# Second inverse's first levels on GpSimd, small products at other steps, opening and end in another order

## The chip, the cores and the metric

The kernel runs on one core of one Trainium2 chip. The metric is the device time of one execution in microseconds (us). The kernel before took 1145.91 us in the median of three runs. A profile is one execution recorded by the hardware; its own time stands in the table below.

Engines go by these names: PE is TensorE (matmuls; PEld is its weight load), DVE is VectorE, ACT is ScalarE, POOL is GpSimd, SP is SyncE, which here only issues transfers. Each engine takes its instructions in the order of its queue; an instruction that waits holds up all that stand behind it on the same engine.

## What is computed

The reference is a model of two layers over 256 tokens of width 2048. The first layer is an RWKV-7 mixer with 32 heads of size 64, the second a sparse attention with 16 heads. Cut to what matters here:

```python
def wkv7_scan(r, w, k, v, a, b):
    def step(S, inp):
        r_t, w_t, k_t, v_t, a_t, b_t = inp
        sa = jnp.einsum('bhvk,bhk->bhv', S, a_t)
        S = S * w_t[:, :, None, :] + sa[..., None] * b_t[:, :, None, :] + v_t[..., None] * k_t[:, :, None, :]
        return S, jnp.einsum('bhvk,bhk->bhv', S, r_t)

def rwkv7_mixer(u, ...):
    xx = token_shift(u) - u
    mixed = u[None] + xx[None] * mu[:, None, None, :]
    rkvz = jnp.einsum('nbtd,nde->nbte', mixed[:4], w_rkvz)
    r, k, v, z = rkvz[0], rkvz[1], rkvz[2], rkvz[3]
    ...
    o = wkv7_scan(rh, heads(decay), kh, vh, -kk, kk * ah)
    ...
    o = (o + bonus) * jax.nn.silu(z)
    return o.astype(u.dtype) @ w_o, v

def reference(x, ...):
    ...
    return rmsnorm(h, final_g)
```

The kernel does not scan token by token. It cuts the 256 tokens into four chunks of 64. Within a chunk the recurrence is a triangular system, so a unit triangular matrix of 64 x 64 has to be inverted for each head and chunk. The kernel inverts its two 32 x 32 diagonal blocks and puts the rest together in the scan.

## The kernel before

All large products are exact to about fp32: each weight and each activation is split into a high part and a low part, and three products are added. The class Weights does this for the weights. SP loads a raw piece (wraw, five buffers), ScalarE copies it to the high part (whi, line 211), VectorE, or GpSimd for some late pieces, takes the difference (wlo, line 190). There are AHEAD + 2 = 5 buffers of whi and wlo, so pieces are made up to five steps ahead, and a new one waits until TensorE has freed a buffer. The activations' parts (mx) are made in split_into: a copy on ScalarE (line 426), a subtraction on VectorE (line 427).

The order of the work: the opening loads x, norms and turns it (lines 357 to 500); then come the values (phase_v), the first block of the gate z, sixteen key blocks (phase_k), the second gate block (phase_z1), the third and fourth (late_z), then the scan over eight units of four heads with the r projection and the output projection laid between, then the second layer, and its last product with the final norm (phase_bo, finish).

A gate block is 512 columns and 16 steps over k; in a step rows_step (lines 583 to 589) issues six matmuls of 512 columns. Each key block j needs small work afterwards: k_norm (a column sum on TensorE at line 732, a root on GpSimd, a copy on ScalarE at line 738), k_turn (two transposes at line 745, then VectorE lines 750 and 751 and GpSimd line 756) and k_close (sixteen small products at line 765, copies on ScalarE, lines 768 and 769, and three stores from SP to the tensor abd). In phase_k these run at step KP = 3 of a later block. What is left after the last key block runs in phase_z1 at the steps of the tuple ZP: at its first step k_close(13), k_turn(14), k_norm(15); at its second k_close(14), k_turn(15); at its third k_close(15).

The inverses are in inverse_load and inverse_ops. There are two, b = 0 for key blocks 0 to 7 and b = 1 for 8 to 15, and each partition holds one 32 x 32 block. inverse_load brings abd to the tile invA, for b = 1 from GpSimd's queue. inverse_ops makes a list of instructions: the identity into invT (memsets, for b = 1 on GpSimd), the 2x2 blocks' corners (a copy of 16 elements), and then levels that double the block: 2 and 4 by products and sums over broadcast views, 8 and 16 by dot products (each a product and a sum over the last axis, on VectorE) after a turn of the upper blocks by ScalarE copies. At the end invT goes to tnd and its transpose to yvd, from where the scan loads them. In the profile all these instructions carry line 824, where op() stands.

What sets the order: a small planner (Sched) walks the phases with a clock of costs and lets generators, the mixes and stage_t among them, run beside them at due times; stage_t issues the inverse's instructions with the pauses given in op(). stage_t(1) starts when key block 15 is closed and the first inverse is out. From this order a scheduler then makes each engine's queue by readiness and rank, except in parts where an engine keeps the written order: the opening (VectorE, ScalarE, GpSimd, TensorE), the key blocks and phase_z1 (TensorE alone), and the scan (TensorE, VectorE, ScalarE, GpSimd, SP). The scan's order is made by the class Deal, which also lays in what is left of the second inverse's list then.

The r mixes (mx from xx) wait for phase_z1's end: their scale is the tile gate, which GpSimd sets to 1.0 there (line 656), after the block's last use of it.

At the end accumulate adds the product to the residual (line 1967), ScalarE squares and sums it (line 1969), and the column's weight is multiplied in (line 1970): on GpSimd for the first four parts of the columns, on VectorE for the last. finish takes the root (VectorE lines 1553 and 1554, GpSimd line 1555), scales the four parts and stores them.

Of the kernel before, what the change touches and what calls it, by code (L numbers as in the profile page):

```python
# [13 lines left out]
OP = mybir.AluOpType  # L14
# [54 lines left out]
HS, HSK = 300, 4  # L69
W1D, CXG = 5, 1  # L70
KPO = 3
KP, ZP = 3, (0, 6, 12)
AUX = {2: ("B0",), 3: ("G",), 4: ("B1",), 5: ("Y",), 7: ("A0",), 8: ("A1",), 9: ("T",)}
AUXL = {2: ("B0",), 3: ("G",), 4: ("B1",), 5: ("Y",), 8: ("T",), 9: ("A0",), 10: ("A1",)}
OPEN = (32, "G", "B0", "B1", 3, "Y", 3, "A0", 2, "A1", 8)
# [149 lines left out]
def hybrid_kernel(ctx: ExitStack, tc: tile.TileContext, a: dict, out: bass.AP):  # L225
# [99 lines left out]
    for ph in QZ:  # L325
        if ph < 10:
            c0 = 128 * QB0[ph]
# [28 lines left out]
    def load_x(tt, c0, c1):  # L356
        nc.sync.dma_start(xt[:, tt, c0:c1], a["x"][0, tt * 128:(tt + 1) * 128, c0:c1])
# [2 lines left out]
    load_x(0, 0, 1024)  # L360
    load_x(0, 1024, 2048)
    load_x(1, 0, 1024)
    load_x(1, 1024, 1536)
    load_x(1, 1536, 2048)
    W.load(1)
    nc.sync.dma_start(prow[0:16, 0, :], g16(a["a_norm_g"][0]))
    nc.sync.dma_start(prow[16:112, 0, :], a["a_mu"][0].rearrange("i (j p) -> (i j) p", p=128))
    nc.sync.dma_start(prow[112:128, 0, :], g16(a["a_k_k"][0]))
    W.load(3)

    def C(name):
# [87 lines left out]
    def scale(tt, c0, c1):  # L459
        sl = xt[:, tt, c0:c1]  # L460
        V.tensor_scalar(sl, sl, rs[:, tt, 1:2], None, op0=OP.mult)
# [7 lines left out]
    if True:  # L469
        turned_x = [accp("tp") for _ in range(2)]  # L470
        S.activation(sq[:, 0:1], half[:, 0:1], AF.Square)
        keep_warm(WARM[0])
        square(0, 0, 1024, 0, S)
        square(0, 1024, 1536, 1, V)
        square(0, 1536, 2048, 2, V)
        rstd0(0)
        square(1, 0, 1024, 0, S)
        square(1, 1024, 1536, 1, V)
        scale(0, 0, 512)
        for kp in range(2):  # L480
            turn_half(turned_x, 0, kp)
        keep_warm(WARM[1])
        square(1, 1536, 1792, 2, V)
        square(1, 1792, 2048, 3, S)
        PE.transpose(pp[:, 0:128], prow[:, 0, :], ident)
        keep_warm(WARM[2])
        rstd0(1)
        W.hold = True
        W.ensure(PRE)
        V.tensor_copy(prm0, pp[:, 0:128])  # L490
        scale(1, 0, 256)
        turn_half(turned_x, 1, 0)
        keep_warm(WARM[3])
        W.low(1)
        scale(1, 256, 512)
        turn_half(turned_x, 1, 1)
        px = turned_x[0]
        for k in range(2):
            norm_x(k, px[:, 256 * k:256 * k + 256], V)
            m = mixed_in("v", k)  # L500
            W.low(1)
            split_into(m, "v", k)
        W.hold = False
# [311 lines left out]
    def inverse_ops(b, A):  # L815
        ops = []
        Tm = late.tile([128, 32, 32], F32, name="invT", bufs=1)
        M1 = late.tile([128, 16, 16], F32, name="invM", bufs=1)
        M2 = late.tile([128, 16, 16], F32, name="invM2", bufs=1)
        X = late.tile([128, 1024], F32, name="invX", bufs=1)  # L820
        PE, V, S, G = Ranked(nc.tensor, "stE"), Ranked(nc.vector, "stE"), Ranked(nc.scalar, "stE"), Ranked(nc.gpsimd, "stE")

        def op(eng, n, fn, *args, pause=0.0, **kw):
            ops.append((eng, n, lambda: fn(*args, **kw), pause))

        flat = Tm.rearrange("p a b -> p (a b)")
        fa = A.rearrange("p a b -> p (a b)")
        op("G" if b else "V", 1024, (G if b else V).memset, Tm, 0.0, pause=500.0)
        op("G" if b else "V", 32, (G if b else V).memset, flat[:, 0::33], 1.0)
        op("V", 16, V.tensor_copy, flat[:, 32::66], fa[:, 32::66], pause=1000.0)  # L830

        def view(t, r0, c0, n, step, rows, colsn, tr=False):
            base = t[:, r0, c0:c0 + 1]
            ap = [list(base.ap[0]), [step * 33, n], [32, rows], [1, colsn]]
            return bass.AP(tensor=base.tensor, offset=base.offset, ap=ap)

        for lv in (2, 4):
            n = 32 // (2 * lv)
            size = n * lv * lv
            m1 = M1.rearrange("p a b -> p (a b)")[:, :size].rearrange("p (n i j) -> p n i j", n=n, i=lv)  # L840
            m2 = M2.rearrange("p a b -> p (a b)")[:, :size].rearrange("p (n i j) -> p n i j", n=n, i=lv)
            x = X[:, :size].rearrange("p (n i j) -> p n i j", n=n, i=lv)
            sh = [128, n, lv, lv]
            for m, first, second in ((m1, lambda k: view(A, lv, k, n, 2 * lv, lv, 1), lambda k: view(Tm, k, 0, n, 2 * lv, 1, lv)),
                                     (m2, lambda k: view(Tm, lv, lv + k, n, 2 * lv, lv, 1), lambda k: m1[:, :, k:k + 1, :])):
                for k in range(lv):
                    op("V", size, V.tensor_tensor, m if k == 0 else x, first(k).to_broadcast(sh), second(k).to_broadcast(sh),
                       op=OP.mult, pause=0.0 if k else DT * 0.25)
                    if k:
                        op("V", size, V.tensor_tensor, m, m, x, op=OP.add, pause=DT * 0.25)  # L850
            op("V", size, V.tensor_copy, view(Tm, lv, 0, n, 2 * lv, lv, lv), m2)

        def dot(out, aa, bb, hb, kk):
            x = X[:, :hb * hb * kk].rearrange("p (i j k) -> p i j k", i=hb, j=hb)
            for i0, i1 in [(0, 4), (4, 8)] if b and hb == 8 else [(0, hb)]:
                sh = [128, i1 - i0, hb, kk]
                n = (i1 - i0) * hb * kk
                op("V", n, V.tensor_tensor, x[:, i0:i1], aa[:, i0:i1, None, :].to_broadcast(sh),
                   bb[:, None, :, :].to_broadcast(sh), op=OP.mult)
                op("V", n, V.tensor_reduce, out[:, i0:i1], x[:, i0:i1], axis=AX.X, op=OP.add,  # L860
                   pause=DT * (0.75 if hb == 8 else 1.0))

        TT = M2.rearrange("p a b -> p (a b)")
        rows = X.rearrange("p (a b) -> p a b", b=32)
        M1f = M1.rearrange("p a b -> p (a b)")
        for lv in (8, 16):
            hb = lv // 2
            Tt = TT[:, :lv * 16].rearrange("p (j k) -> p j k", k=lv)
            Mt = M1f[:, :lv * lv].rearrange("p (j k) -> p j k", k=lv)
            corner = [2 * lv * g for g in range(32 // (2 * lv))]  # L870
            for g, o in enumerate(corner):
                op("S", lv * lv, S.activation, Tt[:, g * lv:g * lv + lv],
                   Tm[:, o:o + lv, o:o + lv].rearrange("p k j -> p j k"), AF.Copy)
            for g, o in enumerate(corner):
                for j0 in (0, hb):
                    for i0 in (0, hb):
                        dot(Mt[:, j0:j0 + hb, i0:i0 + hb].rearrange("p j i -> p i j"),
                            A[:, o + lv + i0:o + lv + i0 + hb, o + j0:o + lv],
                            Tt[:, g * lv + j0:g * lv + j0 + hb, j0:lv], hb, lv - j0)
                for i0 in (0, hb):  # L880
                    for j0 in (0, hb):
                        dot(Tm[:, o + lv + i0:o + lv + i0 + hb, o + j0:o + j0 + hb],
                            Tm[:, o + lv + i0:o + lv + i0 + hb, o + lv:o + lv + i0 + hb],
                            Mt[:, j0:j0 + hb, 0:i0 + hb], hb, i0 + hb)
        op("G", 0, nc.gpsimd.dma_start, tnd[b], Tm)
        for i in range(0, 32, 8):
            op("S", 256, S.activation, rows[:, i:i + 8, :], Tm[:, :, i:i + 8].rearrange("p a b -> p b a"), AF.Copy, pause=700.0)
        op("G", 0, nc.gpsimd.dma_start, yvd[b], rows)
        return ops
# [1075 lines left out]
    def accumulate(tt, ps, c0, cols, i):  # L1965
        hv = tailed(tt, c0, cols)
        V.tensor_tensor(hv, ps, hv, op=OP.add)
        scr = fin.tile([128, 512], F32, name="scr", bufs=2)
        S.activation(scr[:, :cols], hv, AF.Square, accum_out=ssh[:, tt, i:i + 1])
        (G if i < 4 else V).tensor_tensor(hv, hv, tailed(2, c0, cols), op=OP.mult)  # L1970

    def finish(tt):
        rstd(ssh, rsh, tt)
        for i, (c0, c1) in enumerate(((0, 512), (512, 1024), (1024, 1536), (1536, 2048))):
            hv = tailed(tt, c0, c1 - c0)
            if i % 2:
                S.activation(hv, hv, AF.Copy, scale=RS[tt])
            else:
                V.tensor_scalar(hv, hv, RS[tt], None, op0=OP.mult)
            nc.sync.dma_start(out[0, tt * 128:(tt + 1) * 128, c0:c1], hv)  # L1980
# [63 lines left out]
```

## Time and profile before

| what | value |
|---|---|
| time, three runs | 1145.91, 1143.14, 1145.94 us |
| time of the profiled execution | 1146.2 us |
| its span | 1144.4 us |
| mean granted clock of TensorE | 0.989 |
| VectorE, line 190 (wlo), all forms | 616 instructions, 447.3 us |
| ScalarE, line 211 (whi), all forms | 664 instructions, 401.3 us |
| window 260 to 270 us: TensorE, VectorE, GpSimd busy | 9.31, 9.83, 6.14 us |
| window 290 to 300 us: the same | 10.00, 9.78, 2.25 us |
| window 320 to 330 us: the same | 10.00, 8.81, 9.51 us |

How to read it: the span is the time between the first and the last instruction; the execution's time has a little around it. The page has the busy time of each engine and its share of the span. A timeline has the start, the duration, the engine and the line, what is written and from what, and in brackets the idle time before it and who ended it; rows with "x3" are several instructions merged. A window has for each engine the busy microseconds and the number of instructions, then the clock granted to TensorE (1.00 is full speed), the busy share of the transfer engines and GB/s. A row of waits has who waited for whom, the total in us, how often, and the longest. A row of a group has busy time and mean duration in ns, then idle time before it.

### The profile page before, as it was taken

The page shows a single profiled execution, that of the slowest core. Times are in us where ns is not written, and L with a number is a line of the kernel's source. Part 1 is how long each engine was busy: PE and PEld are TensorE (multiplying, and loading weights), DVE is VectorE, ACT ScalarE, POOL GpSimd, SP SyncE. Part 2 cuts the span into 40 slices and gives each one's busy share as a digit, 9 for nine tenths or more (in the row PEclk, how much of TensorE's full clock was granted, in tenths as well). Part 3 has the DMA queues.
Part 4 walks back from the last instruction along what each step waited for, and adds up shares of the span by engine and source line. Part 5 has one row for each costly group of instructions (what it writes and reads, how often), then busy time and mean ns, then how long its engine had stood idle before and what let it go on. Part 6 is the DMA issues. An engine that isn't in the chain of part 4 may idle for free.

```text
span 1144.4 us, 24519 instructions
## 1 busy us (share of the span) xinstructions
PE 1107.3 (97%) x8880; PEld 939.5 (82%) x8880; DVE 869.0 (76%) x1806; ACT 716.1 (63%) x1696; POOL 367.2 (32%) x465
## 2 busy tenths in 40 slices
PE   8999999998999999999999999999999999999996
PEld 7778899987778777777778878787889988898786
DVE  6999976689786997768666876674576888988564
ACT  5667688866745456566556766564656666666553
POOL 1400057766252556653010010100333435352212
PEclk9999999998989999999999999999999999999999
DMA  6558878876898958864457758585656453848552
GB/s 218 174 190 236 247 203 256 241 219 208 245 271 255 237 159 247 211 171 134 131 179 234 225 164 284 160 292 167 188 148 162 122 146 102 203 114 278 164 186 106
DMA packets 239033, 225.35 MB, mean 197 GB/s; under 512 B 58053, under 2 KB 185333, under 8 KB 238912
## 3 DMA queue, kind: packets, MB, share of 16 engines
q1 hardware_dynamic: 233472, 216.65, 64.5%
q0 software_dynamic: 5440, 7.14, 2.4%
q8 instruction: 70, 1.15, 0.5%
q14 instruction: 51, 0.42, 0.1%
HBM read 200.48 MB, written 23.10 MB: 195 GB/s over the span
## 4 chain that ended last, share of the span: by engine, by line
PE 77%; DVE 9%; DMA 4%; issue 4%; POOL 3%; ACT 2%; SPq 0%; ACTq 0%; POOLq 0%; DVEq 0%
PE bank L587 12%; PE bank L589 12%; PE bank L586 12%; PE bank L1337 5%; PE bank L611 5%; DVE wlo L190 3%; PE bank L612 3%; PE bank L241 2%; PE bank L605 2%; PE bank L606 2%; PE bank L607 2%; PE bank L1340 2%; PE pair L1359 2%; PE pair L1361 1%; PE pair L1360 1%
## 5 line engine op out<-in xcount | busy, mean ns | idle before, releaser
L190 DVE TENSOR_TENSOR wlo<-wraw,whi 128x512 fp32r<-128x512 f32 (+2 forms) x616 | 447.3, 741 | 162.4 <-ACT whi L211 159.4
L211 ACT ACTIVATE whi<-wraw 128x512 fp32r<-128x512 f32 (+2 forms) x664 | 401.3, 620 | 241.4 <-PE bank L589 93.0
L587 PE MATMUL bank<-wlo,mx 128*128 128x512 f32 (+3 forms) x576 | 217.4, 379 | 7.4 <-DVE wlo L190 6.5
L589 PE MATMUL bank<-whi,mx 128*128 128x512 f32 (+3 forms) x576 | 215.6, 377 | 0.0
L586 PE MATMUL bank<-whi,mx 128*128 128x512 f32 (+3 forms) x576 | 187.9, 379 | 2.1 <-ACT mx L426 0.9
L587 PEld LDWEIGHTS bank<-wlo,mx 128*128 128x128 f32 x576 | 109.4, 190 | 26.2 <-DVE wlo L190 8.5
L586 PEld LDWEIGHTS bank<-whi,mx 128*128 128x128 f32 x576 | 108.4, 190 | 20.0 <-ACT whi L211 1.5
L589 PEld LDWEIGHTS bank<-whi,mx 128*128 128x128 f32 x576 | 109.3, 190 | 16.7 <-POOL mx L1926 0.4
L1337 PE MATMUL bank<-mx,whi 128*128 128x512 f32 x256 | 102.1, 430 | 0.0
L190 POOL TENSOR_TENSOR wlo<-wraw,whi 128x512 fp32r<-128x512 f32 (+2 forms) x48 | 63.0, 1314 | 110.8 <-ACT whi L211 90.1
L611 PE MATMUL bank<-mx,whi 128*128 128x512 f32 x240 | 86.6, 397 | 0.0
L605 PE MATMUL bank<-mx,whi 128*128 128x256 f32 (+1 forms) x288 | 83.0, 288 | 0.3 <-ACT mx L426 0.3
L606 PE MATMUL bank<-mx,whi 128*128 128x256 f32 (+1 forms) x288 | 81.4, 283 | 0.0
L607 PE MATMUL bank<-mx,wlo 128*128 128x256 f32 (+1 forms) x288 | 81.3, 282 | 0.0
L587 PE MATMUL bank<-wlo,kvh 128*128 128x512 f32 x192 | 76.9, 401 | 0.0
L589 PE MATMUL bank<-whi,kvl 128*128 128x512 f32 x192 | 76.1, 396 | 0.0
L612 PE MATMUL bank<-mx,wlo 128*128 128x256 f32 x256 | 70.6, 285 | 0.2 <-DVE wlo L190 0.2
L1340 PE MATMUL bank<-mx,wlo 128*128 128x256 f32 x256 | 70.7, 284 | 0.0
L586 PE MATMUL bank<-whi,kvh 128*128 128x512 f32 x192 | 67.4, 396 | 0.0
L1337 PEld LDWEIGHTS bank<-mx,whi 128*128 128x128 f32 x256 | 48.0, 189 | 10.6
L605 PEld LDWEIGHTS bank<-mx,whi 128*128 128x128 f32 (+1 forms) x288 | 54.2, 188 | 1.3 <-ACT mx L426 0.7
L607 PEld LDWEIGHTS bank<-mx,wlo 128*128 128x128 f32 (+1 forms) x288 | 54.2, 188 | 0.8 <-DVE wlo L190 0.2
(350 smaller groups left out, 2301.9 us busy)
## 6 DMA issues: line engine op xcount, KB each, us to landing
wraw<-in_a_w_rkvz_dram SPq DMA_DIRECT2D x128, 512.0 KB, 5.2
wraw<-in_kv_w_dram SPq DMA_DIRECT2D x48, 512.0 KB, 4.5
wraw<-in_b_w_in_dram SPq DMA_DIRECT2D x40, 512.0 KB, 4.3
wraw<-in_a_w_o_dram SPq DMA_DIRECT2D x32, 512.0 KB, 4.6
wraw<-in_b_w_o_dram SPq DMA_DIRECT2D x32, 512.0 KB, 4.1
spd<-sp SPq DMA_DIRECT2D x16, 642.0 KB, 5.4
wraw<-in_b_w_in_dram SPq DMA_DIRECT2D x24, 384.0 KB, 3.3
spl<-spd SPq DMA_DIRECT2D x14, 642.0 KB, 7.2
```

The source lines that it names most:

```text
L190: eng.tensor_tensor(lv, src, hv.bitcast(F32), op=OP.subtract)
L211: self.nc.scalar.activation(hv, src, AF.Copy)
L586: PE.matmul(o, mh[:, ts], wh[:, 0, :], start=k == ends[0], stop=False)
L587: PE.matmul(o, mh[:, ts], wl[:, 0, :], start=False, stop=False)
L589: PE.matmul(o, ml[:, ts], wh[:, 0, :], start=False, stop=k == ends[1])
L605: PE.matmul(o, wh[:, s, :], mh, start=k == 0 and first, stop=False, **kw)
L606: PE.matmul(o, wh[:, s, :], ml, start=False, stop=False, **kw)
L607: PE.matmul(o, wl[:, s, :], mh, start=False, stop=k == NK - 1, **kw)
L611: PE.matmul(o, wh[:, s, :], joint[nm, k], start=k == 0, stop=False, **kw)
L612: PE.matmul(o[:, :T], wl[:, s, :], mh, start=False, stop=False, **kw)
L1337: both = lambda: PE.matmul(o, wh[:, s, :], joint["r", k], start=k == 0, stop=k == NK - 1)
L1340: PE.matmul(o[:, :T], wl[:, s, :], mixed["r", k][0], start=False, stop=False)
```

## The change

It has four parts. ZP goes from steps (0, 6, 12) to (3, 8, 13) of the second gate block. In inverse_ops the first copy and all of levels 2 and 4 take the engine el/eng: GpSimd for b = 1, VectorE for b = 0 as before. In the opening the three parameter loads (prow) go ahead of the last two loads of x, the first weight load is no longer issued by itself ahead of them, and the scaling of the second token half's first columns stands ahead of the copy of the turned parameters (prm). At the end, the last part's weight is multiplied in after the root's VectorE instructions and not before them.

```diff
-KP, ZP = 3, (0, 6, 12)
+KP, ZP = 3, (3, 8, 13)
...
     load_x(1, 0, 1024)
-    load_x(1, 1024, 1536)
-    load_x(1, 1536, 2048)
-    W.load(1)
     nc.sync.dma_start(prow[0:16, 0, :], g16(a["a_norm_g"][0]))
     nc.sync.dma_start(prow[16:112, 0, :], a["a_mu"][0].rearrange("i (j p) -> (i j) p", p=128))
     nc.sync.dma_start(prow[112:128, 0, :], g16(a["a_k_k"][0]))
+    load_x(1, 1024, 1536)
+    load_x(1, 1536, 2048)
     W.load(3)
...
         W.ensure(PRE)
+        scale(1, 0, 256)
         V.tensor_copy(prm0, pp[:, 0:128])
-        scale(1, 0, 256)
         turn_half(turned_x, 1, 0)
...
         op("G" if b else "V", 32, (G if b else V).memset, flat[:, 0::33], 1.0)
-        op("V", 16, V.tensor_copy, flat[:, 32::66], fa[:, 32::66], pause=1000.0)
+        el, eng = ("G", G) if b else ("V", V)
+        op(el, 16, eng.tensor_copy, flat[:, 32::66], fa[:, 32::66], pause=1000.0)
...
                 for k in range(lv):
-                    op("V", size, V.tensor_tensor, m if k == 0 else x, ...
+                    op(el, size, eng.tensor_tensor, m if k == 0 else x, ...
                        op=OP.mult, pause=0.0 if k else DT * 0.25)
                     if k:
-                        op("V", size, V.tensor_tensor, m, m, x, op=OP.add, pause=DT * 0.25)
-            op("V", size, V.tensor_copy, view(Tm, lv, 0, n, 2 * lv, lv, lv), m2)
+                        op(el, size, eng.tensor_tensor, m, m, x, op=OP.add, pause=DT * 0.25)
+            op(el, size, eng.tensor_copy, view(Tm, lv, 0, n, 2 * lv, lv, lv), m2)
...
-        (G if i < 4 else V).tensor_tensor(hv, hv, tailed(2, c0, cols), op=OP.mult)
+        weigh = lambda: (G if i < 4 else V).tensor_tensor(hv, hv, tailed(2, c0, cols), op=OP.mult)
+        if i < 4:
+            weigh()
+        else:
+            last[tt] = weigh
+
+    last = {}
 
     def finish(tt):
         rstd(ssh, rsh, tt)
+        last[tt]()
```

More of the change, by code (lines that the diff above doesn't have):

```diff
@@ L846, in inverse_ops @@
                 for k in range(lv):
-                    op("V", size, V.tensor_tensor, m if k == 0 else x, first(k).to_broadcast(sh), second(k).to_broadcast(sh),
+                    op(el, size, eng.tensor_tensor, m if k == 0 else x, first(k).to_broadcast(sh), second(k).to_broadcast(sh),
                        op=OP.mult, pause=0.0 if k else DT * 0.25)
                     if k:
-                        op("V", size, V.tensor_tensor, m, m, x, op=OP.add, pause=DT * 0.25)
-            op("V", size, V.tensor_copy, view(Tm, lv, 0, n, 2 * lv, lv, lv), m2)
+                        op(el, size, eng.tensor_tensor, m, m, x, op=OP.add, pause=DT * 0.25)
+            op(el, size, eng.tensor_copy, view(Tm, lv, 0, n, 2 * lv, lv, lv), m2)
         def dot(out, aa, bb, hb, kk):
```

## The prediction

> **What bounds the kernel now.** I read the page first, then the waits of TensorE, the windows of ten microseconds, and last the timelines of the engines around the two places where TensorE stood still. Page, waits and two windows:
>
> ```profile
> span 1144.4 us, 24519 instructions
> PE 1107.3 (97%) x8880; PEld 939.5 (82%) x8880; DVE 869.0 (76%) x1806; ACT 716.1 (63%) x1696; POOL 367.2 (32%) x465
> ...
> PE bank L587 <- DVE wlo L190: 6.5, 5, 4.8
> ...
> 270.00:280.00 10.00, 7.10 (x55) 5.89 (x55) 10.00 (x16) 6.53 (x17) 5.98 (x7) 0.84 0.59 181
> 310.00:320.00 10.00, 4.92 (x15) 3.39 (x15) 5.36 (x20) 6.41 (x15) 2.43 (x6) 0.71 1.00 319
> ```
>
> TensorE is the bound: 1107.3 of 1144.4 us, so a change pays only where it stands still or runs slowly. The two windows are such places, with 2.9 and 5.1 us of idle time and granted clocks of 0.84 and 0.71. In the first, VectorE is busy for all 10.00 us; in the second it is idle for nearly half. Both lie where the change works: the second gate block (k steps of six matmuls) and the block behind it. The one long wait of the whole run, 4.8 us on wlo, is in the second.
>
> The first place, on TensorE, then on VectorE:
>
> ```profile
> 274.00 0.39 PE L589 MATMUL bank<-whi,mx 128*128 128x512 f32 x1
> 276.33 0.46 PE L765 MATMUL bank<-sp 64*64 64x64 f32 x16 [1.95 <-DVE sp L751]
> 277.56 0.69 PE L745 MATMUL bank<-cst,rnx 128*128 128x128 f32 x2 [0.76 <-ACT rnx L738]
> 278.44 1.01 PE L732 MATMUL bank<-cst,t 128*128 128x2 f32 x4 [0.19 <-ACT t L724]
> 279.31 0.77 PE L586 MATMUL bank<-whi,mx 128*128 128x512 f32 x1
> ...
> 283.07 0.43 PE bank L589
> 283.82 0.24 PE bank L587
> ...
> 276.11 0.68 DVE L190 TENSOR_TENSOR wlo<-wraw,whi 128x512 fp32r<-128x512 f32 x1
> 277.84 0.68 DVE L190 TENSOR_TENSOR wlo<-wraw,whi 128x512 fp32r<-128x512 f32 x1
> ```
>
> After step 0 the small products wait 1.95 + 0.76 + 0.19 = 2.90 us for VectorE and ScalarE. Then the matmuls go at one per 0.43 us until about 283.7, and at 0.24 (0.23 in most) after. Ten of them lie between 279.31 and 283.7: 4.35 us instead of 2.3, so 2.05 lost to the clock. This place costs 2.90 + 2.05 = 4.95.
>
> The second place, on TensorE, VectorE, ScalarE and GpSimd:
>
> ```profile
> 311.88 0.73 PE L586 MATMUL bank<-whi,mx 128*128 128x512 f32 x2 [0.32 <-ACT whi L211]
> 317.38 0.80 PE L587 MATMUL bank<-wlo,mx 128*128 128x512 f32 x1 [4.77 <-DVE wlo L190]
> 321.27 0.40 PE L589 MATMUL bank<-whi,mx 128*128 128x512 f32 x1
> ...
> 307.54 3.83 DVE L427 TENSOR_TENSOR mx<-xx,mx 128x256 fp32r<-128x256 f32 x10
> 316.01 0.18 DVE L824 COPY invT<-invA 128x16 f32<-128x16 f32 x1 [4.64 <-DMA invA<-abd]
> 316.64 0.69 DVE L190 TENSOR_TENSOR wlo<-wraw,whi 128x512 fp32r<-128x512 f32 x1
> 330.06 0.29 DVE L824 COPY invT<-invM 128x64 f32<-128x64 f32 x1
> ...
> 306.80 4.51 ACT L426 ACTIVATE mx<-xx,gate 128x256 fp32r<-128x256 f32 x11
> 311.22 0.61 ACT L211 ACTIVATE whi<-wraw 128x512 fp32r<-128x512 f32 x1
> 312.54 0.61 ACT L211 ACTIVATE whi<-wraw 128x512 fp32r<-128x512 f32 x1
> 314.25 1.65 ACT L211 ACTIVATE whi<-wraw 128x512 fp32r<-128x512 f32 x3
> ...
> 305.57 1.17 POOL L824 MEMSET invT<- 128x1024 f32 x2 [3.09 <-DMA tnd<-invT]
> 306.65 0.10 POOL L656 MEMSET gate<- 128x1 f32 x1
> 308.74 1.06 POOL L812 DMA_DIRECT2D invA<-abd  x2 [1.99 <-DMA abd<-abs]
> ```
>
> VectorE reaches the first copy of the second inverse (invT<-invA) and stands for 4.64 us until the load of invA has landed. Behind it in VectorE's queue is the wlo for which TensorE waits 4.77. The whi for that wlo had been ready since 311.22 + 0.61 = 311.8. TensorE idles 0.32 + 4.77 = 5.09, and nine matmuls then take 321.27 - 317.38 = 3.89 us, where nine at 0.23 take 2.1: 1.8 more. This place costs 6.9.
>
> **The change, part by part.** The sum is made against the profiled execution: span 1144.4, time 1146.2, thus 1.8 outside the span; the median of the runs, 1145.91, is 0.3 below it.
>
> **Small products at steps 3, 8, 13.** Nothing is added, three groups move. At step 3 the products' inputs are old (the last one came at 278.44). But VectorE was busy throughout, so the weights of steps 2 and 3 become the next to be late. As I count the wlo instructions, the row at 276.11 belongs to step 2, done at 276.8, and that at 277.84 to step 3, done at 278.5. TensorE would end step 0 at 274.2, step 1 at 275.6, want the wlo of step 2 at 275.85 and wait 0.95, then want that of step 3 at 278.15 and wait 0.35. So 1.3 stays, if VectorE keeps its order: 4.95 - 1.3 = 3.65 gained. The ends are 0 (VectorE spends the block at its limit, and what is gained is paid back in waits on wlo) and 4.95. The last group moves by one step of 1.4 us, which delays abd and so invA, though the block runs 3.65 earlier: invA lands between 2.3 us earlier and at the old time. No one on TensorE waits for that directly.
>
> The Trainium skill (TensorE: Matmul & The Clock Gate, "What's actually happening") puts the fall to half rate after an idle window of about 3.4 us. Here idle pieces of 1.95 and 0.76 with little work between them sufficed. By the page two waits under 1 us leave the clock alone and the sum stands; should they cost it as the rows' pieces did, 2.05 are to be taken off.
>
> **The second inverse's 2x2 and 4x4 levels on GpSimd.** 23 instructions leave VectorE: the first copy; for the 2x2 level six of 128x32 and a copy; for the 4x4 level fourteen of 128x64 and a copy. With them goes the wait for invA: GpSimd takes it. Behind the waiting copy on GpSimd stand the memsets of the scan's tiles and the loads for its first heads, which only the scan, two gate blocks later, wants: nothing. VectorE's wlo then follows whi: done near 311.8 + 0.6 = 312.4, against 316.64 + 0.69 before. What is late next is whi, behind the eleven mix copies of the row at 306.80: TensorE waits 0.32 for it, 0.5 for the wlo, and 0.35 at the third whi (314.25 + 0.52 + 0.6 = 315.4, wanted at 312.4 + 2 x 1.4 - 0.1 = 315.1). So 1.2 stays: 6.9 - 1.2 = 5.7 gained. Of the 23 instructions' own time on VectorE I count nothing; it has slack there.
>
> No row shows GpSimd at such small operands. The nearest are these:
>
> ```profile
> L1040 POOL COPY pc<-spl 128x4 f32<-128x4 f32 x16 | 4.1, 284 | 0.2
> L756 POOL TENSOR_TENSOR sp<-f,pinv 64x256 f32<-64x256 f32 x32 | 30.2, 942 | 26.4 <-DVE f L726 25.2
> ...
> 282.08 1.94 POOL L756 TENSOR_TENSOR sp<-nk,an 64x256 f32<-64x256 f32 x2
> ...
> 283.36 1.22 DVE L190 TENSOR_TENSOR wlo<-wraw,whi 128x512 fp32r<-128x512 f32 x1
> ```
>
> An instruction costs 0.28 to 0.94; by size nearer to the first, I take 0.45. The chain is 23 x 0.45 = 10.4 us (6.4 to 21.7). On VectorE it took 330.06 + 0.29 - 316.01 = 14.3, because it was interleaved with wlo. So it ends 4 us earlier (8 earlier to 7 later), and that is worth nothing by itself: the following levels on VectorE fill gaps. A loss is possible, see the third rival. The last two rows show GpSimd holding VectorE up: a wlo of 0.69 takes 1.22 beside L756. Twenty-three holds of 0.45 would be 10 us of VectorE, spread over a stretch in which TensorE has four of the five weight buffers (AHEAD + 2) in hand, 4 x 1.4 = 5.5 us: taken at nothing, 2 at the far end.
>
> **Opening and end.**
>
> ```profile
> 4.40 0.44 SPq L366 DMA_DIRECT2D prow<-in_a_norm_g_dram  x1
> 5.59 0.31 SPq L368 DMA_DIRECT2D prow<-in_a_k_k_dram  x1
> ...
> DMA to landing us min/median/max: 4.4/5.2/6.0
> ...
> 13.17 0.29 DVE L490 COPY prm<-bank 128x128 f32<-128x128 f32 x1 [1.91 <-PE bank L485]
> 13.38 0.34 DVE L461 TENSOR_SCALAR xt<-xt,rs 128x256 f32<-128x256 f32 x1
> 13.78 0.48 PE L456 MATMUL bank<-cst,xt 128*128 128x128 f32 x2 [0.22 <-DVE xt L461]
> ...
> 1137.46 0.42 DVE L1970 TENSOR_TENSOR mx<-mx,mx 128x256 f32<-128x256 f32 x1 [0.64 <-ACT scr L1969]
> 1138.22 0.55 POOL L1555 TENSOR_TENSOR rsh<-rsh,half 128x1 f32<-128x1 f32 x1 [5.08 <-DVE rsh L1554]
> ```
>
> The scaling of xt no longer stands behind a copy that waits for TensorE; the transposes that waited 0.22 for it then follow TensorE's own queue: 0.2 gained. The three parameter loads go ahead of the last quarter of x on SP's queue: 5.59 + 0.31 - 4.40 = 1.5 us later issue for that quarter and the first weights. The landing row of x (4.4 to 6.0) says that later loads wait for earlier ones by 1.6, which covers it; uncovered it costs up to 1.5. At the end the last weighting (0.42) leaves the chain from the square to the root and runs beside the root's 0.55: 0.35 gained, since the instruction behind it overlaps it a little; the bounds are 0 and 0.42.
>
> **Sum:** 3.65 + 5.7 + 0.2 + 0.35 = 9.9; 1146.2 - 9.9 = 1136.3.
>
> **Rivals.**
>
> *One stall takes the place of the other.* ScalarE's eleven mix copies start at 306.80, right after the memset of gate at 306.65, which stood behind a memset that waited 3.09 us for a store of the first inverse. If that order on GpSimd stays, the copies end at 311.3 however early TensorE comes; it meets the whi 3.65 us sooner and idles that long, loses the clock (1.8), and the gain is 5.7 - 1.8 + 0.55 = 4.5: 1141.7. For it: the first inverse ends where VectorE's full queue lets it. Against: the gate's own release comes earlier too, and may go first.
>
> *The change does not do what it says in the gate block.* VectorE at 10.00 of 10 decides the pace, the 3.65 come back as waits on wlo: 9.9 - 3.65 = 6.25, 1139.9. For it speaks the 10.00; against, that weights are made five pieces ahead.
>
> *Slower: ScalarE waits for GpSimd.* The next level begins with two copies on ScalarE that read GpSimd's last result; all later whi stand behind them. If the scheduler puts them as early as 320 and invA lands at 316.01, with x us per instruction ScalarE stands 316 + 23x - 320; 5.5 is covered, 1.8 of clock comes on top. At 0.94 that is 21.6 - 4 - 5.5 + 1.8 = 13.9: 9.9 - 13.9 = 4 slower, 1150.2. It turns the sign at 23x = 17.6, x = 0.77. The Trainium skill (SBUF — State Buffer, "Who interferes with whom") speaks for it: VectorE with two SBUF inputs and GpSimd reading SBUF shut each other out for a whole instruction. The trace agrees (the 1.22 above); by that rule the forecast ends nearer 0.7 than 0.45 per instruction. Between, at 0.6 to 0.77, hardly anything is left of the gain.
>
> **How the numbers follow.** About 0.3%, 3.4 us, is what a measurement of this kernel can tell from no change, so faster means below 1142.5. Forecast 0.52; first rival 0.18; second 0.12; the third's middle, no change, 0.10; slower 0.08. The first rival is so near the border that 0.03 of it counts as no change. Faster is then 0.52 + 0.15 + 0.12 = 0.79, same 0.13, slower 0.08. The range goes from both stalls gone without remainder (9.9 + 1.3 + 1.2 = 12.4: 1133.8, a little under it, 1133, for the bounds of opening and end) to 1143, past the first rival.
>
> **What would show it.** Right: no wait before L765, L745 and L732 in the gate block; no idle time on VectorE for invA; both windows above 9 us of TensorE with a clock of 1.00; 23 GpSimd instructions of L824 of some 0.45; the scaling of xt ahead of the copy of prm; the last weighting beside the root. Wrong: whi waited for behind the mix copies for more than 2 us (first rival), several waits on wlo between 275 and 300 (second), ScalarE idle before its copies from invT (third), or waits in the scan, whose order is laid out anew if another number of the inverse's instructions is left for it; for that I have no row and take nothing.

## The result and the profile after

The kernel after takes 1138.82 us in the median of four runs (1137.99 to 1139.74), the kernel before beside it 1145.78 (1143.14 to 1145.94, four runs). The ratio is 0.9945 with a 95% interval of 0.9928 to 0.9962: 7.0 us faster in the medians. On another chip, with the experiments, it was 0.9956 (0.9940 to 0.9973; 1140.21 of seven runs against 1144.77 of twelve). The forecast was 1136.3, faster. The profiled execution took 1138.34.

The page of after, its span and its engines:

```profile
span 1136.2 us, 24517 instructions
...
PE 1103.1 (97%) x8880; PEld 936.3 (82%) x8880; DVE 860.8 (76%) x1783; ACT 714.3 (63%) x1696; POOL 382.2 (34%) x488
```

VectorE has 23 instructions fewer (1806 before), GpSimd 23 more (465). TensorE's span is 8.2 us shorter, its busy time 4.2: the rest is waiting. Its waits, in all and the longest:

```profile
PE bank L585 <- ACT whi L211: 2.4, 3, 1.3
PE bank L764 <- POOL sp L755: 2.2, 4, 0.9
PE bank L586 <- DVE wlo L190: 2.0, 4, 0.9
PE bank L744 <- ACT rnx L737: 1.1, 1, 1.1
```

The wait of 4.8 us on wlo is gone. In its place stand waits of 0.7 to 1.3 us on three engines. (Line numbers of after from 400 to 823 are one lower than those of before.) Four windows of after:

```profile
270.00:280.00 10.00, 9.01 (x63) 7.02 (x61) 10.00 (x15) 6.86 (x17) 6.03 (x7) 1.00 0.58 183
...
310.00:320.00 10.00, 9.24 (x39) 7.34 (x40) 8.38 (x16) 7.34 (x15) 6.25 (x14) 1.00 1.00 257
320.00:330.00 10.00, 9.41 (x40) 6.94 (x39) 2.59 (x4) 3.28 (x6) 9.21 (x19) 1.00 1.07 263
...
350.00:360.00 10.00, 9.26 (x54) 7.84 (x52) 9.45 (x27) 4.90 (x10) 2.82 (x4) 1.00 0.99 302
```

The two windows of the prediction are above 9 us of TensorE at a clock of 1.00 (before: 7.10 at 0.84 and 4.92 at 0.71). New are the lower two: TensorE is short of 10.00 there, VectorE does 9.45 us of work at 350, and the transfer engines are full from 310 to 330. The rows behind this, from the timeline of after on TensorE, VectorE, ScalarE and GpSimd:

```profile
276.61 0.50 PE L586 MATMUL bank<-wlo,mx 128*128 128x512 f32 x1 [0.93 <-DVE wlo L190]
289.33 0.44 PE L744 MATMUL bank<-cst,rnx 128*128 128x128 f32 x2 [1.14 <-ACT rnx L737]
297.09 0.33 PE L764 MATMUL bank<-sp 64*64 64x64 f32 x2 [0.49 <-POOL sp L755]
297.89 0.46 PE L764 MATMUL bank<-sp 64*64 64x64 f32 x14 [0.47 <-POOL sp L755]
310.76 0.73 PE L585 MATMUL bank<-whi,mx 128*128 128x512 f32 x2 [1.31 <-ACT whi L211]
325.54 0.73 PE L585 MATMUL bank<-whi,mx 128*128 128x512 f32 x2 [0.59 <-ACT whi L211]
357.47 0.39 PE L1340 MATMUL bank<-mx,wlo 128*128 128x256 f32 x1 [0.74 <-DVE wlo L190]
...
351.09 0.28 DVE L823 TENSOR_TENSOR invX<-invA,invM 128x128 f32<-128x128 f32 x1
354.32 0.68 DVE L190 TENSOR_TENSOR wlo<-wraw,whi 128x512 fp32r<-128x512 f32 x1
...
305.28 4.91 ACT L425 ACTIVATE mx<-xx,gate 128x256 fp32r<-128x256 f32 x12 [0.68 <-POOL gate L655]
324.86 1.15 ACT L211 ACTIVATE whi<-wraw 128x512 fp32r<-128x512 f32 x2 [6.03 <-DMA wraw<-in_a_w_rkvz_dram]
350.18 0.53 ACT L823 ACTIVATE invM<-invT 128x64 f32<-128x64 f32 x2
...
304.25 0.96 POOL L823 MEMSET invT<- 128x1024 f32 x1 [3.40 <-DMA tnd<-invT]
311.17 1.16 POOL L956 DMA_DIRECT2D spl<-spd  x2
318.98 0.65 POOL L823 COPY invT<-invA 128x16 f32<-128x16 f32 x1 [3.50 <-DMA invA<-abd]
...
319.80 2.28 POOL L922 DMA_DIRECT2D a<-abd  x4
...
337.57 0.30 POOL L823 TENSOR_TENSOR invX<-invA,invT 128x64 f32<-128x64 f32 x1
...
338.68 0.64 POOL L823 TENSOR_TENSOR invX<-invA,invT 128x64 f32<-128x64 f32 x1
...
345.61 0.24 POOL L823 COPY invT<-invM 128x64 f32<-128x64 f32 x1
```

In the gate block the first group of small products (step 3) waits for nothing; the wait of 0.93 us at 276.61 is one for a weight. The second and third group wait 1.14 and 0.49 + 0.47. The 23 GpSimd instructions take 10.6 us together (0.46 each), but are spread from 318.98 to 345.85, with the issues of other loads between them. The next level begins with two copies on ScalarE, at 350.18; its dots then stand on VectorE in a row from 351.09, ahead of the weight that TensorE wants at 357. At 324.86 ScalarE has waited 6.03 us for a raw weight.

**Where the time went.** The kernels issue the same 8880 matmuls. The start of a matmul in before's trace less the start of the matmul with the same number in another trace says how far that kernel is ahead. Counted from 0, I take number 1760 (269.48 us in before), 1960 (307.78, end of the gate block), 2000 (324.26, behind the prediction's second place), 2320 (371.50, in the scan) and 4000 (468.24). So the bounds of a stretch are times of before; a kernel that is ahead passes them that much earlier on its own clock. After is ahead by 0.29, 2.12, 7.62, 5.34 and 7.31 us there, so the stretches give +1.83, +5.50, -2.28 and +1.97. The table has this for all kernels; a minus is time lost against before.

| kernel | 269 to 308 | 308 to 324 | 324 to 371 | 371 to 468 | ratio to before (95%) |
|---|---|---|---|---|---|
| after | 1.83 | 5.50 | -2.28 | 1.97 | 0.9945 (0.9928 to 0.9962) |
| after_again | 1.83 | 5.42 | -1.79 | 0.66 | 0.9956 (0.9940 to 0.9973) |
| before_again | 0.03 | 0.20 | 0.00 | -0.65 | (one run) |
| e1_small | 1.82 | 2.24 | -0.01 | 1.44 | 0.9984 (0.9969 to 0.9999) |
| e2_pool | -0.13 | 6.44 | 0.00 | -0.44 | 0.9967 (0.9952 to 0.9983) |
| e3_ends | 0.80 | -0.15 | 0.00 | -0.24 | 1.0015 (0.9998 to 1.0031) |
| e4_gate | 1.84 | 5.90 | -1.40 | -1.27 | 0.9961 (0.9944 to 0.9978) |
| small_3_10_15 | 3.91 | 2.30 | -1.49 | 1.21 | 0.9957 (0.9942 to 0.9972) |
| chain_first | 1.85 | 5.52 | -0.62 | 1.02 | 0.9929 (0.9917 to 0.9942) |
| spl_first | 2.47 | 5.29 | 0.00 | 2.14 | 0.9927 (0.9913 to 0.9942) |
| spl_first_gate | 2.46 | 5.89 | -1.32 | 2.04 | 0.9929 (0.9908 to 0.9949) |
| spl_gate_3_10_15 | 4.50 | 2.41 | -0.03 | 0.70 | 0.9944 (0.9925 to 0.9962) |

In the first column up to 0.8 us can be chance: e3_ends has the old steps and still 0.80, with a granted clock of 0.91 from 270 to 280 us where before has 0.84, and spl_first and spl_first_gate have 0.6 more than the other kernels with steps 3, 8, 13, though nothing of the block was edited in them.

The end, before and then after, on the timeline:

```profile
1136.40 0.42 DVE L1967 TENSOR_TENSOR mx<-bank,mx 128x256 f32<-128x256 f32 x1 [2.34 <-PE bank L2011]
1138.80 1.33 ACT L1977 ACTIVATE mx<-mx,rsh 128x512 f32<-128x512 f32 x2 [1.38 <-POOL rsh L1555]
```

```profile
1127.84 0.42 DVE L1967 TENSOR_TENSOR mx<-bank,mx 128x256 f32<-128x256 f32 x1 [2.47 <-PE bank L2018]
1128.98 0.42 DVE L1970 TENSOR_TENSOR mx<-mx,mx 128x256 f32<-128x256 f32 x1
1129.31 0.15 DVE L1554 TENSOR_SCALAR rsh<-rsh 128x1 f32<-128x1 f32 x1
1130.12 1.33 ACT L1984 ACTIVATE mx<-mx,rsh 128x512 f32<-128x512 f32 x2 [1.25 <-POOL rsh L1555]
```

From the last sum to the scaling it takes 2.28 us instead of 2.40. The weighting (line 1970) was put between the root's two VectorE instructions, not behind them.

### The profile page after: what moved, and what is told of

Read it like the earlier page. It is cut to its first block, busy times and chain, and to the rows that moved or that the text cites. A ratio compares the mean times of both kernels' runs of the same rounds, so it can differ in the third digit from the quotient of the medians.

```text
span 1136.2 us, 24517 instructions
## 1 busy us (share of the span) xinstructions
PE 1103.1 (97%) x8880; PEld 936.3 (82%) x8880; DVE 860.8 (76%) x1783; ACT 714.3 (63%) x1696; POOL 382.2 (34%) x488
## 4 chain that ended last, share of the span: by engine, by line
PE 74%; DVE 10%; DMA 7%; issue 4%; ACT 3%; POOL 1%; SPq 1%; ACTq 0%; POOLq 0%; DVEq 0%
PE bank L586 11%; PE bank L588 11%; PE bank L585 11%; PE bank L1337 5%; PE bank L610 5%; DVE wlo L190 3%; PE bank L611 3%; PE bank L604 2%; PE bank L605 2%; PE bank L606 2%; PE bank L241 2%; DMA wraw<-in_a_w_rkvz_dram 2%; PE bank L1340 2%; PE pair L1359 2%; PE pair L1361 1%
## 5 line engine op out<-in xcount | busy, mean ns | idle before, releaser
L604 PE MATMUL bank<-mx,whi 128*128 128x256 f32 (+1 forms) x288 | 84.3, 293 | 0.3 <-ACT mx L425 0.3
L605 PE MATMUL bank<-mx,whi 128*128 128x256 f32 (+1 forms) x288 | 82.7, 287 | 0.0
L604 PEld LDWEIGHTS bank<-mx,whi 128*128 128x128 f32 (+1 forms) x288 | 55.6, 193 | 1.3 <-ACT mx L425 0.7
L605 PEld LDWEIGHTS bank<-mx,whi 128*128 128x128 f32 (+1 forms) x288 | 55.7, 193 | 0.5
```

Source lines behind the costliest of these rows:

```text
L604: PE.matmul(o, wh[:, s, :], mh, start=k == 0 and first, stop=False, **kw)
L605: PE.matmul(o, wh[:, s, :], ml, start=False, stop=False, **kw)
```

## The experiments

My theory after the two traces: the two stalls went as forecast, but what came free was partly taken up by what had been just hidden behind them: the inputs of the later small products, the mix copies on ScalarE, the raw weights, and the dots on VectorE. The rivals: the parts' gains add up and the difference is chance (clock, scan), or one part brings all of it.

**One part alone.** e1_small is before with one edit:

```diff
-KP, ZP = 3, (0, 6, 12)
+KP, ZP = 3, (3, 8, 13)
```

> The kernel before with the small products at steps 3, 8 and 13 alone. Theory A (what the trace of after shows: 4.7 us ahead after the first group, of which the second and third group's new waits and the late weights give 2.9 back inside the block): TensorE is 3 to 4 us ahead behind step 3, about 1.8 ahead at the block's end, and since the wait of 4.8 us for the wlo behind invA is still there in the next block, some of the 1.8 is lost to it again: 0 to 1.8 us faster in all. Theory B (the prediction): the block gains 3.65 and keeps it, 3 to 4 us faster. Theory C: the wait for invA follows the third group, one step later, and eats everything: 0 or up to 1 us slower.

1141.67 against 1143.78, ratio 0.9984 (0.9969 to 0.9999). The gate block gives 1.82, as in after, so theory A holds there and B falls. The next block gave 2.24 more, which none of the three had: the wait for invA is still on VectorE, but in another place. The timeline of e1_small on TensorE and VectorE, then two windows:

```profile
318.60 0.50 PE L587 MATMUL bank<-wlo,mx 128*128 128x512 f32 x1 [2.90 <-DVE wlo L190]
...
317.67 0.22 DVE L824 COPY invT<-invA 128x16 f32<-128x16 f32 x1 [3.82 <-DMA invA<-abd]
```

```profile
310.00:320.00 10.00, 6.58 (x26) 4.79 (x27) 6.08 (x17) 6.01 (x13) 8.31 (x17) 1.00 1.01 286
320.00:330.00 10.00, 10.00 (x46) 8.28 (x45) 7.29 (x25) 4.50 (x9) 6.61 (x14) 1.00 1.03 237
```

The copy now stands three wlo later in VectorE's queue, TensorE waits 2.90 instead of 4.77 us, and the clock stays at 1.00. Moving the small products thus takes off part of the second stall as well.

e2_pool is before with the 23 instructions on GpSimd alone (the diff's lines with el and eng):

> The kernel before with the second inverse's first copy and its 2x2 and 4x4 levels on GpSimd alone. Theory A (forecast): the wait of 4.8 us for wlo goes and with it 1.8 us of lower clock, 1.2 stays: 5.7 us ahead behind that block; by the trace of after 1.3 is then lost to late loads of wraw and 0.95 at the start of the r stage to VectorE's late dots, so 3 to 4.5 us faster at the end. Rival B: the gain of after in this block needs the small products' earlier gate block; with the old one TensorE comes to the mix copies as before, and 2 us or less are gained. Rival C: the 23 instructions run at 0.7 us or more beside VectorE and ScalarE waits for them: slower.

1139.99, ratio 0.9967 (0.9952 to 0.9983). The next block gives 6.44, more than the 5.7 forecast, and nothing is given back before 371: the forecast's mechanism is right by itself, B and C fall, and so does what theory A took over from the trace of after, the losses near 325 and at the r stage. Each part alone gives 4.06 and 6.31 from 269 to 324; both together gave 7.33 and 7.25, not 10.4. They overlap: e1_small shrinks the same wait, and with both TensorE comes early enough to meet the mix copies. The timeline of GpSimd and ScalarE in e2_pool:

```profile
314.44 0.69 POOL L824 COPY invT<-invA 128x16 f32<-128x16 f32 x1 [5.93 <-DMA invA<-abd]
319.25 1.17 POOL L957 DMA_DIRECT2D spl<-spd  x2
345.34 0.24 POOL L824 COPY invT<-invM 128x64 f32<-128x64 f32 x1
...
346.25 0.52 ACT L824 ACTIVATE invM<-invT 128x64 f32<-128x64 f32 x2
```

Here the large loads (spl) are issued at 319.25, not 311.17 as in after. The chain of the 23 instructions ends at 345.58, as late as in after (345.85), and yet the r stage loses nothing: ScalarE's two copies follow at 346.25, and the dots begin at 347.07 with wlo between them. In after the same two copies stand behind other copies in ScalarE's queue until 350.18. So a late chain alone does not cost the 0.95 us; it takes a late place in ScalarE's queue as well.

e3_ends is before with the opening's and the end's order alone:

> The kernel before with the opening's and the end's new order alone. By the trace of after: TensorE starts 0.3 us earlier, the end is 0.1 us shorter: 0.4 to 0.5 us faster, less than the runs differ. By the prediction 0.2 + 0.35 = 0.55. Rival: the later quarter of x costs up to 1.5 us in some executions: slower by up to 1.0. If the waits of the scan or of the clock fall otherwise than before though nothing there is changed, the scan's 1.3 to 2 us in the trace of after are no part of the change.

1145.27, ratio 1.0015 (0.9998 to 1.0031): no gain that can be measured, and a loss of up to 3.5 us is inside the interval. Its first large matmul starts at 15.62 us against 16.26 in before, but in the second trace of before it starts at 15.44: the two traces of one kernel differ by more than what was forecast. The trace shows 0.12 at the end and nothing sure in the opening. What these edits are worth in the time stays open: the interval leaves 0.2 us of gain to 3.5 of loss, so the rival, a later quarter of x that makes some executions up to 1.0 slower, is not ruled out, and a part of what after lacks may be theirs.

**The gate's memset on VectorE** (e4_gate: after, with this edit):

```diff
-        G.memset(t, value)
+        V.memset(t, value)
```

> The kernel after, with the one-element-wide memset of the gate for the second layer's mixes written by VectorE instead of GpSimd, so that it no longer stands behind the memset of invT that waits 3.4 us for the store of the first inverse. Theory A (my first rival's mechanism is still in the kernel after, at a third of its price): the mix copies start up to 2.5 us earlier (302.6 rather than 305.3), the wait of 1.31 us for whi behind them goes, and TensorE is 1.0 to 1.3 us ahead of after at 320; 0 to 1.3 us faster at the end. Theory B: the loads of wraw are the limit from 310 on (DMA share 1.0 and more, 1.34 us lost at 325 in after): TensorE waits for them that much longer, and the time is that of after within 0.3 us.

1139.16, ratio 0.9961 (0.9944 to 0.9978), the time of after. The timeline of ScalarE and TensorE:

```profile
303.50 2.90 ACT L425 ACTIVATE mx<-xx,gate 128x256 fp32r<-128x256 f32 x7
...
309.89 0.73 PE L585 MATMUL bank<-whi,mx 128*128 128x512 f32 x2 [0.89 <-ACT whi L211]
```

The mixes start 1.8 us earlier and the wait for whi falls from 1.31 to 0.89: 0.4 to 0.5 gained in the block. So my first rival's mechanism, the gate behind the memset that waits for a store, is at work in after, at a price of half a microsecond, not four. The rest of the wait belongs to ScalarE, which is busy for 10.00 us of the window from 300.

**After again**, for its time on another chip and a second trace:

> The kernel after, unchanged, beside the three below: its time on the same chip, and a second trace. If the stages in which after lost time again are its own, they come back at the same places: TensorE late by 1.3 us at the wraw loads about 325, by 0.95 at the start of the r stage, and 1.8 gained in the second gate block. What does not come back (the clock of the key blocks, of the scan) is chance. Time 1137 to 1140.

What is its own came back (1.83 and 5.42 gained; 0.80 lost by 342 us and 0.99 at the r stage), and the scan gave 0.66, not 1.97. Two rows of its timeline, TensorE and ScalarE:

```profile
356.29 0.39 PE L1340 MATMUL bank<-mx,wlo 128*128 128x256 f32 x1 [0.73 <-DVE wlo L190]
...
323.55 1.15 ACT L211 ACTIVATE whi<-wraw 128x512 fp32r<-128x512 f32 x2 [5.38 <-DMA wraw<-in_a_w_rkvz_dram]
```

**The order on GpSimd.** chain_first puts the first heads' loads behind the inverse's chain (inv_t keeps invT; the require waits until the planner has issued the chain):

```diff
-ZHOOK = (2, 4)
+ZHOOK = (6, 4)
...
+                sch.require(lambda: 1 in rest and len(rest[1]) <= total[1] - 25)
+                for t in [s[:, 0:1] for s in SPL0] + [t[:, 0, 0, 0:1] for t in (A10, T00, Yb[0])]:
+                    G.tensor_copy(t, inv_t[1][:, 4, 0:1])
                 for x in range(2):
                     G.dma_start(SPL0[x][:, :SPW], spd[x])
```

> The kernel after, with a one-column copy from the second inverse's last GpSimd result into the tiles spl, a, t and Yb of the first heads, ahead of their loads and memsets: GpSimd then runs its 23 instructions in one go and issues those loads behind them, about 10 us later. Theory A (queue neighbours): the chain ends about 329 instead of 345.9, VectorE's dots lie ahead of the r stage, the 0.95 us there go, and the loads no longer compete with wraw at 325, so the 1.34 us there go too: 2 to 2.3 us ahead of after at 366, 1.5 to 2.3 faster at the end if the scan's first heads are not late. Rival B: the loads come too late for the scan's first heads and TensorE waits for them at 366 to 370: no gain, or slower. Rival C: the wraw wait has to do with the whole traffic and only moves: 0.95 gained.

1137.17, ratio 0.9929 (0.9917 to 0.9942). The loss from 324 to 371 falls from 1.79 to 0.62, and TensorE waits for no load at 366 to 370 that the profile names (B falls, but for 0.67 us at 366.67 before a product on spl, for which the profile names no releaser). The timeline of GpSimd, VectorE, ScalarE and TensorE:

```profile
317.02 0.70 POOL L826 COPY invT<-invA 128x16 f32<-128x16 f32 x1 [2.40 <-DMA invA<-abd]
...
326.16 0.24 POOL L826 COPY invT<-invM 128x64 f32<-128x64 f32 x1
327.18 1.16 POOL L963 DMA_DIRECT2D spl<-spd  x2
...
326.78 0.29 DVE L826 TENSOR_TENSOR invX<-invA,invM 128x128 f32<-128x128 f32 x1 [3.46 <-ACT invM L826]
...
319.62 1.38 ACT L211 ACTIVATE whi<-wraw 128x512 fp32r<-128x512 f32 x2 [1.34 <-DMA wraw<-in_a_w_rkvz_dram]
326.43 0.53 ACT L826 ACTIVATE invM<-invT 128x64 f32<-128x64 f32 x2 [3.83 <-POOL invT L826]
...
331.95 0.51 PE L586 MATMUL bank<-wlo,mx 128*128 128x512 f32 x1 [0.28 <-DVE wlo L190]
```

The chain takes 9.4 us in one go, the dots of the 8x8 level run from 326.78 between the wlo of the late_z block instead of in a row at 351, and the r stage waits for nothing. With spl behind the chain, the copy of whi that waits 6.03 and 5.38 us in the two traces of after waits 1.34. The 0.62 that remain are lost at 331.3 to 332.3 us, on wlo. Ahead of that ScalarE stood 3.83 us for GpSimd's last result and VectorE 3.46 behind it: this is the wait of the prediction's third rival, and the weights made ahead cover all of it but this.

spl_first leaves spl ahead of the chain (the same edit without the SPL0 copies, and with the spl loads ahead of the require):

> As chain_first, but the two spl loads stay ahead of the chain, where after has them; only a, t and Yb come behind it. If the spl loads are what made wraw late, the 1.34 us at 325 stay and only the 0.95 at the r stage go: about 0.95 ahead of after at 366. If a, t and Yb made it late, both go, as in chain_first. If the wraw loss stays and the dots' loss too, the order on GpSimd is not the cause of either.

1136.95, ratio 0.9927 (0.9913 to 0.9942). Nothing is lost from 324 to 371. By my expectation a, t and Yb would then be the cause of the late weights, but ScalarE's row says otherwise:

```profile
322.09 1.15 ACT L211 ACTIVATE whi<-wraw 128x512 fp32r<-128x512 f32 x2 [4.43 <-DMA wraw<-in_a_w_rkvz_dram]
```

The late weight is there, only a little less late. Put beside what TensorE loses from 324 to 342 us, this wait reads: 4.43 us, nothing lost; 4.91 (spl_gate_3_10_15), 0.03; 4.92 (small_3_10_15), 0.04; 5.30 (e4_gate), 0.42; 5.38 (after_again), 0.80; 6.03 (after), 1.34; 6.06 (spl_first_gate), 1.28. By these rows the pieces made ahead cover about 4.9 us of it; beyond that TensorE pays. The edits of chain_first and spl_first differ in the place of spl alone, and the same copy waits 1.34 and 4.43: spl makes the weights late, and whether that costs anything is decided by fractions of a microsecond.

**Later small products.** small_3_10_15 is after with ZP = (3, 10, 15):

> The kernel after, with the small products of the second gate block at steps 3, 10 and 15 instead of 3, 8 and 13. Theory A: in after, the second and third group come before VectorE, ScalarE and GpSimd have their inputs (TensorE waits 1.14 and 0.96 us); two steps of 1.4 us later they find them ready, and the block gains 3.5 to 4 us over before rather than 1.8. Rival B: VectorE sets the pace of the block (10.00 of 10 busy), the waits come back at wlo, and the block's gain stays at 1.8. Rival C: the block gains, but abd and with it invA come 2.8 us later and the next block or the chain on GpSimd gives it back: the time of after within 0.3 us.

1139.74, ratio 0.9957 (0.9942 to 0.9972), the time of after. The waits of the second and third group are gone and the gate block gives 3.91, close to the 3.65 of the prediction; the next block gives 2.30 instead of 5.5. The timeline of TensorE and one window:

```profile
308.39 0.73 PE L585 MATMUL bank<-whi,mx 128*128 128x512 f32 x2 [2.87 <-ACT whi L211]
```

```profile
310.00:320.00 10.00, 10.00 (x39) 8.03 (x38) 7.46 (x14) 6.38 (x13) 7.50 (x17) 0.83 0.96 264
```

This is the first rival with both its parts: what the gate block gains is waited for behind the mix copies (2.87 us, where the rival had 3.65), and the clock is lost on top. It is rival C with ScalarE in the place of invA. VectorE's limit (B) is not what binds.

**A second trace of before:**

> The kernel before, unchanged, for a second trace of it. What is its own must come back: the waits of 1.95 and 0.76 us and the lower clock in the second gate block, the wait of 4.8 us for wlo behind invA, no wait at the start of the r stage. What is chance may differ: the clock about 460 in the scan (0.83 in the first trace), the key blocks before 270.

1145.51 us. Both stalls are back, and the clock in the scan fell too; TensorE's row and one window:

```profile
315.67 0.80 PE L587 MATMUL bank<-wlo,mx 128*128 128x512 f32 x1 [4.65 <-DVE wlo L190]
```

```profile
460.00:470.00 10.00, 10.00 (x172) 7.97 (x173) 8.02 (x15) 5.42 (x15) 8.15 (x15) 0.84 0.79 167
```

Between 269 and 371 its two traces differ by 0.2 us, ahead of that by 1.3, in the scan by 0.65. Differences of that size outside the changed stretch say nothing about the change, and e3_ends shows 0.8 by chance inside it.

**Both mends together.** spl_first_gate has spl_first's edit and e4_gate's:

> spl_first with the gate's memset on VectorE: both mends in one. Theory: the mix copies start about 1.8 us earlier, the wait for whi behind them falls from 1.3-1.5 to 0.9, and the losses at 325 and at the r stage stay away: TensorE 0.4 to 0.6 us ahead of spl_first at 366; time 1136 to 1137. Rival: the earlier mixes are paid for by late weights as in the kernel with the gate alone (0.4 lost at 333): the time of spl_first.

1136.57 against 1145.03, ratio 0.9929 (0.9908 to 0.9949): the rival's answer. The block gains 0.6 over spl_first, and the weights take it back (1.32 lost, ScalarE's wait 6.06).

spl_gate_3_10_15 has the later steps as well:

> spl_first_gate with the small products at steps 3, 10 and 15. Theory A: what the two blocks together can give is bounded by ScalarE, which copies weights and mixes without a pause from 300 to 311; the waits that go inside the gate block come back as a longer wait for whi behind the mix copies (2.9 us and a lower clock when tried on the kernel after): TensorE not ahead of spl_first_gate at 324, or behind by up to 1.3. Theory B: the gate's memset was what held the mixes: with it on VectorE the 2 us gained in the gate block stay, 1.5 to 2 us ahead at 324, and the time is 1134 to 1135.

1138.76, ratio 0.9944 (0.9925 to 0.9962). The gate block gives 4.50, the next one 2.41. The timeline of TensorE:

```profile
307.51 0.77 PE L585 MATMUL bank<-whi,mx 128*128 128x512 f32 x2 [2.90 <-ACT whi L211]
```

Theory A: with the gate out of the way the wait is still 2.90, and ScalarE is busy for 10.00 us of the window from 300. That its copies bound the two blocks together, and that the steps 3, 8, 13 lie near what they allow, fits this; no run with fewer copies shows it.

## Why the prediction was right, and where its sizes were off

*Direction and mechanism* held: both stalls went, for the reasons given, and none of the three rivals decided the time. The forecast of 9.9 us stands against 7.0 and 4.6 in the two comparisons; in the two traces the stretch from 269 to 371 gained 5.1 and 5.5, where the two large terms of the sum had 9.35. That the first comparison lies nearer to the forecast is in part luck: in its trace 1.97 us come from the scan, which no part of the change was to speed up, and the second trace has 0.66 there.

*Small products, 3.65:* measured 1.83. The residue at the first group was near (1.3 forecast in two waits, 0.95 and 0.35; 0.93 measured in one). The mis-sized step is "Nothing is added, three groups move": only the first group was checked for its inputs. The second and third meet inputs that are not ready, 1.14 and 0.96 us. The run with steps 10 and 15 shows that a price of 3.9 was there to be had in this block, and that it would not have lasted.

*"invA lands between 2.3 us earlier and at the old time":* wrong. Its first reader starts at 318.98 and 317.85 in the two traces of after, against 316.01: GpSimd issued the load at 310.14 and 309.50 rather than 308.74, and it took longer to land (7.0 to 8.2 us, 6.2 to 6.6 in before). TensorE did not wait for it, as the prediction said.

*Two waits under 1 us leave the clock alone:* so it was; the window from 270, with the wait of 0.93, has 1.00.

*Second inverse, 5.7:* measured 5.50 and 5.42 in its block, 6.44 alone. The residue (1.2) was there as one wait of 1.31 and 1.40 for whi. Right.

*"So it ends 4 us earlier ... and that is worth nothing by itself":* this step failed. The price per instruction was right (0.45 forecast, 0.46 and 0.42 measured in the two traces of after), but I reckoned the 23 instructions in one go and took what stands behind the first of them for harmless, as nobody wants it before the scan. The scheduler laid the loads of the first heads between them; the chain ended at 345.85, 15 us later than the levels did in before (330.35). ScalarE's copies for the next level fell behind others, and the dots came in a row ahead of the r stage: 0.95 and 0.99 lost. (e2_pool, with as late a chain but these copies in time, loses nothing.) The loads themselves, 2 x 642 KB at 311, made raw weights late as soon as TensorE ran on without a stall: 1.34 and 0.80 lost. Together 2.28 and 1.79, which the sum has at zero; chain_first and spl_first take them off, wholly or in greater part, by the order alone. Of the 4.3 and 3.9 us by which the two terms were forecast too high, this is about half.

*Opening 0.2, end 0.35:* the end is 0.12, since the weighting went between the root's instructions, where it still delays the second. In the opening the scaling runs ahead of the copy as forecast, but two traces of one kernel differ there by more than 0.2.

*Rivals.* One stall in the place of the other: its mechanism is at work, at half a microsecond, and small_3_10_15 shows it at nearly full size. VectorE as the bound: no. ScalarE waiting for GpSimd: not in after, where the chain's lateness was paid on VectorE instead; in chain_first ScalarE does wait 3.83 us for it, nearly all of it covered. (In that rival's text 0.6 us per instruction leaves, by its own sum, 9.9 - (13.8 - 4 - 5.5 + 1.8) = 3.8 us of the gain, which is not "hardly anything".) The Trainium skill (SBUF — State Buffer, "Who interferes with whom") has an instruction of VectorE with two SBUF inputs and one of GpSimd that reads SBUF shut each other out. The trace agrees in kind: the same 128x64 product takes 0.30 us at 337.57 and 0.64 at 338.68, the second while VectorE is in a wlo. The mean stayed at 0.46; that VectorE is not always in such an instruction would explain it, but was not counted.

*What stays open.* The first experiments' chip had before at 1143.78 us in 35 runs, against 1144.77 to 1145.78 elsewhere; e1_small and e2_pool gain 2 to 2.5 us less there in the medians than in the traces' stretches, and why is not settled. In the scan the kernels differ by up to 2 us, with a lower clock or without. Behind 468 us the trace of after gains another 1.25; 0.94 of it lies between 1092 and 1127, where e1_small, which changes nothing there, gains as much and after_again gains nothing.

## What to carry to other kernels

Two stalls that lie one behind the other are not two gains: ask, for the engine that is freed, who is next late at the new pace, and price the next two, not one. When work moves to another engine, its duration is the small question; the large one is what stands between its instructions in that queue, and what the transfers among them take from the weights. What came of the order of that queue alone (spl_first, chain_first) is 3 us more than the change in the medians of one chip, 1.2 to 1.8 of it in the stretch from 324 to 371. And a result that comes late costs only where its readers stand late in their queues too (e2_pool).

## What the runs showed of the hardware

A wait does not by its length say whether the clock falls. TensorE's waits of 4.65 and 4.77 us went with windows of 0.66 and 0.71; one of 2.87 with 0.83 (small_3_10_15), one of 2.90 with 0.90 and 0.93 (spl_gate_3_10_15, windows from 300 and 310); another of 2.90 with no fall (e1_small, 1.00 in both windows). In the scan one of 2.29 went with 0.83 (before, at 459 us) and one of 2.89 with none (after, at 453). The Trainium skill (TensorE: Matmul & The Clock Gate, "What's actually happening") names an idle window of about 3.4 us that runs freely, so that its phase decides. The free phase fits waits of one length with and without a fall; a window that must be idle for 3.4 us does not fit a fall after 2.87 or 2.29, and here the runs decide.

Tiny products on GpSimd (128x32, 128x64) take either 0.25 to 0.32 us or 0.63 to 0.80 in the chain of after, with no value between; 23 instructions of such sizes in one go took 9.4 us (chain_first).
